# Sixteen accumulating weight transfers moved from the attention part into the recurrence of a hybrid residual block

## The chip, the cores and the metric

The kernel runs on one core of a Trainium2 chip. The metric is the device time of one execution in microseconds (us), lower is better. Five engines work in parallel, each with an instruction stream of its own: TensorE (PE in the profile, PEld for its weight loads), VectorE (DVE), ScalarE (ACT), GpSimd (POOL) and SyncE (SP). SP, ACT and POOL also issue DMA transfers. An instruction that has to wait for a semaphore holds up everything behind it on its engine.

## The reference, cut to what matters

One residual block over 1024 tokens of width 1024, in float32:

```python
xn = rmsnorm(x, norm1_g[layer])
u = xn @ w_in[layer]          # q,k,v (3x512), f,i,q,g of HGRN2 (4x512), two gates (2x1024)
...
o_sb = stick_breaking_attention(q_sb, k_sb, v_sb)                    # 8 heads of 64
o_hg = rmsnorm(hgrn2(silu(q_hg), k_hg, i_hg, log_f), hg_norm_g) * silu(g_hg)   # 4 heads of 128
g_a = sigmoid(gate_sb + bg[:D_MODEL])
g_b = sigmoid(gate_hg + bg[D_MODEL:])
merged = g_a * (o_sb @ w_o_sb) + g_b * (o_hg @ w_o_hg)
h = x + merged @ w_out
h = h + square(relu(rmsnorm(h, norm2_g) @ w_ff1)) @ w_ff2
return rmsnorm(h, final_g)
```

## The kernel before, in words

Everything is one long program on one core. Float32 products are made of three matmuls on a high and a low part, so most operands are split first: ACT copies the high part (`hi_copy`, line 157), DVE subtracts it from the original (`lo_sub`, line 162). All matmuls go through one helper (line 129), transposes through another (132).

Several large products (gates, output projections, MLP) are computed by Strassen-like schemes with fewer block products, which need sums of weight blocks. Some of these sums are made ahead by DMA alone, in HBM: a transfer on POOL's queue copies one block to a scratch tensor, and a later one adds a second block to it (`accum_op`). There are three such sets, each a Python generator that issues one transfer per step:

- `out_weight_sums`: four sums of W_OUT in `tw`, 16 copies and then 16 adds of 256 KB (line 1365);
- `sb_weight_sums`: four sums of W_OSB in `tv`, 8 transfers of 512 KB (line 1629), where the third and the fourth sum are built on `tv[1]` and the one made from it;
- `gate_weight_sums`: the gates' fourth sum in `tg4` (called `tg` in the profile), the sum of four blocks of W_IN: 4 copies and 12 adds of 512 KB (line 1377). It is read by SP's loads of the units `wga0` to `wga7`, much later.

The stages in order: norm and transposes of x (0 to 80 us), attention (about 80 to 326 us), the HGRN2 recurrence (about 323 to 550 us), gates, output projection, MLP.

**Attention** is a loop over 64 items (8 heads, 8 query blocks each). In each item ACT computes `rm`, the sigmoid of the scores (line 840), two items ahead; DVE scans it (859); PE transposes it to `pw`; ACT and DVE split that to `wTh` and `wTl`; PE multiplies with the values (`po`), and ACT evacuates to `osb` (934). Matmuls of the projections fill PE in between (`st.advance`). Beside that, `input_sums` lets DVE build sums of the input in `xs`, which POOL's queue stores to `sx` (1538); tiles of 128x1024 (`rm` of the larger blocks, `xs`, weights and others) share one pool of 40 slots, so a new `rm` can wait until the store of an old `xs` has landed. POOL also issues the transfers that copy QH and QL to the other partitions (730) and, once per head, an add of the two halves of `osb` (941); it also clears parts of `wTh` and `wTl` (892). SP stores `osb` of the last head to `od` (952).

At each item the chain of the three sets takes one step, `if i % 16 != 0: next(wsums, None)`; each transfer is placed behind `scored[0]`, the latest sigmoid of the scores, by an ordering that asks for no semaphore (`NOSYNC`): it only says where the instruction stands.

**The recurrence** goes over four heads. `hg_levels(h)` does seven levels of halves; each level ends with the product of the decays, `hg_level[0] = mul(right, right, left)` (DVE, line 170, `pp<-pp` in the profile), and PE computes the level's scores `sl` from keys `ksl` and `q`. `hg_tail(h)` computes the outputs; POOL makes the inverse roots from `hss` there (266, 270), and DVE multiplies by them (`hon`). PE is filled with projections again: first `pji` from W_IN's columns of `i`, whose weight comes in four quarters `wir`, loaded by SP and split to `wih` and `wil`.

Of the kernel before, what the change touches and what calls it, by code (L numbers as in the profile page):

```python
# [16 lines left out]
AX = mybir.AxisListType  # L17
PSUM = bass.MemoryType.PSUM
NOSYNC = mybir.DependencyInfo(mybir.DependencyClass.NoSync, mybir.DependencyReason.DATA)

P = 128
T = 1024
# [18 lines left out]
def kernel(  # L41
# [19 lines left out]
    nc = tc.nc  # L61
# [32 lines left out]
    def dram(name, shape):  # L94
        return scratch.tile(shape, F32, tag=name, name=name)
# [10 lines left out]
    def after(ins, earlier):  # L106
        if earlier is not None and earlier.ins is not ins.ins:
            tc.add_manual_dep(ins.ins, earlier.ins.name, NOSYNC, reason="issue order")
        return ins
# [710 lines left out]
    turn_lo, scored = [None], [None]  # L820

    def scores(h, qb):
        open_block("main")
        nk = (qb + 1) * P
        QH, QL, KS = qk[h]
        rm = zs[h, qb] = slot_n(f"rm{h}_{qb}", nk)
        step = 320 if nk == 640 else 512
        for s0 in range(0, nk, step):
            m = min(nk - s0, step)
            n = max(m, 256)  # L830
            z = bank(f"z{h}_{qb}_{s0}")
            for i, Q in enumerate((QH, QL)):
                matmul(
                    z[:, :n],
                    Q[:, qb * P : (qb + 1) * P],
                    KS[:, s0 : s0 + n],
                    start=i == 0,
                    stop=i == 1,
                )
            scored[0] = nc.scalar.activation(  # L840
                rm[:, s0 : s0 + m], z[:, :m], AF.Sigmoid, scale=-0.125
            )
# [7 lines left out]
    def weights(h, qb):  # L850

        nk = (qb + 1) * P
        rm = zs[h, qb]
        parts = ((512, nk), (0, 512)) if qb == NT - 1 else ((0, nk),)
        for i, (a, b) in enumerate(parts):
            rr = rm[:, a:b][:, ::-1]
            sc = nc.vector.tensor_tensor_scan(  # L859
                out=rr,  # L860
                data0=rr,
                data1=bits[:, 1024 - nk + a : 1024 - nk + b][:, ::-1],
                initial=rm[:, b : b + 1] if i else 0.0,
                op0=ALU.mult,
                op1=ALU.max,
            )
            if (h, qb) == items[0]:
                after(sc, masked[0])
            if i == 1 or (qb == 5 and h in (2,)):
                after(sc, turn_lo[0])  # L870
# [85 lines left out]
    hg_sum, hg_level = [None], [None]  # L956
# [397 lines left out]
    def out_block(i, j):  # L1354
        return W_OUT[i * 512 : (i + 1) * 512, j * 512 : (j + 1) * 512]

    def out_weight_sums():
        b11, b12, b21, b22 = (out_block(i, j) for i in range(2) for j in range(2))
        plain = ((1, b11), (3, b12), (2, b22), (4, b21))
        summed = ((1, b12), (3, b22), (2, tw[1]), (4, tw[2]))  # L1360
        for op, ways in ((ALU.bypass, plain), (ALU.add, summed)):
            for i, src in ways:
                for r in range(4):
                    rs = slice(r * P, (r + 1) * P)
                    after(nc.gpsimd.dma_start(tw[i][rs], src[rs], accum_op=op), scored[0])
                    yield

    tg4 = dram("tg4", [512, D])

    def gate_weight_sums():  # L1370
        for op, i, c0 in (
            (ALU.bypass, 0, C_GA), (ALU.add, 0, C_GB), (ALU.add, 1, C_GA), (ALU.add, 1, C_GB),
        ):
            for r in range(4):
                rs = slice(r * P, (r + 1) * P)
                src = W_IN[i * 512 + r * P : i * 512 + (r + 1) * P, c0 : c0 + D]
                after(nc.gpsimd.dma_start(tg4[rs], src, accum_op=op), scored[0])
                yield

    def gate_bias(which, cb):  # L1380
# [150 lines left out]
    def input_sums():  # L1531


        def step(out, a, b, op):
            after(nc.vector.tensor_tensor(out=out, in0=a, in1=b, op=op), turn_lo[0])

        def stored(m, kp, t):
            nc.gpsimd.dma_start(sx[m][kp], t)

        for kp in range(2):  # L1540
            (h00, l00), (h01, l01), (h10, l10), (h11, l11) = (
                [t.bitcast(F32) for t in xn.t[i, 2 * j + kp]] for i in range(2) for j in range(2)
            )
            s = slot(f"xs{kp}")
            step(s, h00, h10, ALU.subtract)
            yield
            step(s, s, l00, ALU.add)
            yield
            step(s, s, l10, ALU.subtract)
            stored(7, kp, s)  # L1550
            yield
            yield
            step(s, s, h11, ALU.add)
            yield
            after(
                nc.vector.scalar_tensor_tensor(
                    out=s, in0=s, scalar=-1.0, in1=l11, op0=ALU.mult, op1=ALU.subtract
                ),
                turn_lo[0],
            )  # L1560
            stored(6, kp, s)
            s4 = slot(f"xs4{kp}")
            yield
            step(s4, s, h01, ALU.add)
            yield
            step(s4, s4, l01, ALU.add)
            stored(3, kp, s4)
            yield
            step(s, s, h00, ALU.add)
            yield  # L1570
            step(s, s, l00, ALU.add)
            stored(5, kp, s)
            yield
# [41 lines left out]
    def sb_block(i, j):  # L1615
        return W_OSB[i * 256 : (i + 1) * 256, j * 512 : (j + 1) * 512]

    def sb_weight_sums():
        for t, op, src in (
            (1, ALU.bypass, sb_block(0, 0)),  # L1620
            (3, ALU.bypass, sb_block(0, 1)),
            (1, ALU.add, sb_block(0, 1)),
            (3, ALU.add, sb_block(1, 1)),
            (2, ALU.bypass, tv[1]),
            (2, ALU.add, sb_block(1, 1)),
            (4, ALU.bypass, tv[2]),
            (4, ALU.add, sb_block(1, 0)),
        ):
            after(nc.gpsimd.dma_start(tv[t], src, accum_op=op), scored[0])
            yield  # L1630
# [1005 lines left out]
    n_first = 4  # L2636
    n_fill = n_first + 14 * NHS
    ready = deque()
    wsums = chain(out_weight_sums(), sb_weight_sums(), gate_weight_sums())
    insums = input_sums()  # L2640
    done = 0
    for i, it in enumerate(items):
        if i + 1 < len(items):
            weights(*items[i + 1])
        if i + 2 < len(items):
            st.finish(j_qk[items[min(i + 4, len(items) - 1)][0]])
            scores(*items[i + 2])
        if i < 2:
            v_moves()
        if i % 16 != 0:  # L2650
            next(wsums, None)
        if i > 2 and i % 5 > 1:
            next(insums, None)
        want = n_first + (i + 1) * (n_fill - n_first) // len(items)
        st.advance(want - done, j_q[2])
        done = want
        before = ready.popleft() if ready else None

        def between():
            if before:  # L2660
                values(*before)

        r = turn(*it, between)
        if i == len(items) - 2:
            attended[0] = turn_lo[0]
        if it[1] != NT - 1:
            between()
        if r:
            ready.append(r)
# [9 lines left out]
    for h in range(NHG + 1):  # L2679
        lev = hg_levels(h) if h < NHG else iter(())  # L2680
        tail = hg_tail(h - 1) if h > 0 else iter(())
        upto = (j_i, j_sb[0], j_raw[1], j_raw[6], j_held)[h]
        going, turned = True, False
        while going:
            going = False
            for g in (lev, tail):
                if g is tail and h == 1 and turned and going and st.pos < j_i:
                    continue
                turned = turned or g is tail
                if next(g, StopIteration) is not StopIteration:  # L2690
                    going = True
                    owed += FILL[h]
                    for step in range(int(owed)):
                        st.advance(1, upto)
                        while soon:
                            soon.pop(0)()
                    owed -= int(owed)
        if h + 1 < NHG:
            st.finish(max(j_f[h + 1], j_q[h + 1]))
# [102 lines left out]
```

## Time and profile before

| | us |
|---|---|
| median of 3 runs | 1419.32 (1418.46 to 1420.83) |
| the profiled execution, its own time | 1421.75 |
| its span, first to last instruction | 1420.0 |
| PE busy | 1406.0 (99%) |
| DVE busy | 1066.9 (75%) |
| ACT busy | 667.8 (47%) |
| POOL busy | 164.4 (12%) |
| mean granted clock of PE | 0.997 |

Times in the views are counted from the span's start. A timeline row reads: start, busy time, engine, line, operation, output<-inputs, shape, count, and in square brackets how long the engine had stood idle before it and what ended that. In a view of one tile, a transfer's row gives its issue (duration, first and last start), and the line on landing the time from issue to landing. PEclk is the clock that the throttle granted, 1.00 being full speed.

### The profile page before, as it was taken

The page shows a single profiled execution, that of the slowest core. Times are in us where ns is not written, and L with a number is a line of the kernel's source. Part 1 is how long each engine was busy: PE and PEld are TensorE (multiplying, and loading weights), DVE is VectorE, ACT ScalarE, POOL GpSimd, SP SyncE. Part 2 cuts the span into 40 slices and gives each one's busy share as a digit, 9 for nine tenths or more (in the row PEclk, how much of TensorE's full clock was granted, in tenths as well). Part 3 has the DMA queues.
Part 4 walks back from the last instruction along what each step waited for, and adds up shares of the span by engine and source line. Part 5 has one row for each costly group of instructions (what it writes and reads, how often), then busy time and mean ns, then how long its engine had stood idle before and what let it go on. Part 6 is the DMA issues. An engine that isn't in the chain of part 4 may idle for free.

```text
span 1420.0 us, 18679 instructions
## 1 busy us (share of the span) xinstructions
PE 1406.0 (99%) x6824; PEld 1181.1 (83%) x6824; DVE 1066.9 (75%) x1463; ACT 667.8 (47%) x1147; POOL 164.4 (12%) x318
## 2 busy tenths in 40 slices
PE   9999999999999999999999999999999999999997
PEld 8888788888888888888888888888888888888886
DVE  6678887668578968987788897676666657768765
ACT  6455455554244555433334754445444443433343
POOL 3023343310001111000000300000000000000041
PEclk9999999999999999999999999999999999999999
DMA  7357778864213668364585514444346964776824
GB/s 252 83 141 201 150 142 195 211 149 134 86 56 105 215 222 264 129 215 156 165 294 194 185 59 164 163 163 149 137 143 244 355 255 160 270 278 241 282 91 176
DMA packets 169556, 258.18 MB, mean 182 GB/s; under 512 B 31404, under 2 KB 92376, under 8 KB 169432
## 3 DMA queue, kind: packets, MB, share of 16 engines
q1 hardware_dynamic: 148280, 196.15, 40.9%
q0 software_dynamic: 16320, 50.34, 13.8%
q10 hardware_dynamic: 4864, 10.49, 2.1%
q8 instruction: 54, 0.88, 0.3%
q14 instruction: 38, 0.31, 0.1%
HBM read 186.69 MB, written 84.94 MB: 191 GB/s over the span
## 4 chain that ended last, share of the span: by engine, by line
PE 95%; DVE 1%; ACT 1%; DMA 1%; issue 1%; SPq 0%; POOL 0%; POOLq 0%; DVEq 0%
PE pm L129 21%; PE pX L129 9%; PE pW L129 6%; PE pY L129 6%; PE pjqk L129 5%; PE gY L129 4%; PE gX L129 4%; PE pga L129 4%; PE pjf L129 3%; PE pji L129 3%; PE pyh L129 3%; PE pjq L129 3%; PE pys L129 3%; PE po L129 3%; PE pwX L129 2%; PE z L129 2%
## 5 line engine op out<-in xcount | busy, mean ns | idle before, releaser
L859 DVE TENSOR_TENSOR_SCAN rm<-rm,bits 128x512 f32<-128x512 f32 (+6 forms) x72 | 87.4, 1221 | 29.7 <-ACT rm L840 28.8
L157 ACT CAST whid<-w 128x1024 fp32r<-128x1024 f32 x30 | 31.6, 1054 | 154.1 <-PE pm L129 83.2
L129 PE MATMUL pm<-whid,sh 128*128 128x512 f32 x240 | 93.4, 389 | 0.0
L129 PE MATMUL pm<-wlod,sh 128*128 128x512 f32 x240 | 93.4, 389 | 0.0
L129 PE MATMUL pm<-whid,sl 128*128 128x512 f32 x240 | 93.4, 389 | 0.0
L129 PE MATMUL pm<-tl,sh 128*128 128x512 f32 (+1 forms) x210 | 81.3, 387 | 0.0
L129 PE MATMUL pm<-th,sl 128*128 128x512 f32 (+1 forms) x210 | 81.3, 387 | 0.0
L129 PE MATMUL pm<-th,sh 128*128 128x512 f32 (+1 forms) x210 | 81.3, 387 | 0.0
L162 DVE TENSOR_TENSOR wlod<-w,whid 128x1024 fp32r<-128x1024 f32 x30 | 36.7, 1223 | 53.6 <-ACT whid L157 53.6
L157 ACT CAST wTh<-pw 128x512 fp32r<-128x512 f32 (+2 forms) x96 | 43.8, 483 | 57.9 <-PE pw L132 54.2
L2413 POOL TENSOR_SCALAR fss<-fss 128x1 f32<-128x1 f32 x8 | 4.4, 552 | 562.0 <-ACT fsc L2408 561.5
L162 DVE TENSOR_TENSOR sl<-sa,sh 128x1024 fp32r<-128x1024 f32 x56 | 68.3, 1219 | 0.4 <-ACT sh L157 0.3
L162 DVE TENSOR_TENSOR wTl<-pw,wTh 128x512 fp32r<-128x512 f32 (+2 forms) x96 | 50.4, 546 | 21.8 <-ACT wTh L157 20.7
L157 ACT CAST sh<-sa 128x1024 fp32r<-128x1024 f32 x56 | 57.2, 1046 | 9.0 <-DMA sa<-ad 9.0
L129 PEld LDWEIGHTS pm<-wlod,sh 128*128 128x128 f32 x240 | 45.1, 188 | 9.5
L129 PEld LDWEIGHTS pm<-whid,sl 128*128 128x128 f32 x240 | 45.1, 188 | 9.3
L129 PEld LDWEIGHTS pm<-whid,sh 128*128 128x128 f32 x240 | 45.0, 187 | 9.4
L129 PE MATMUL pX<-sqh,t1l 128*128 128x512 f32 x128 | 49.9, 390 | 0.0
L129 PE MATMUL pX<-sql,t1h 128*128 128x512 f32 x128 | 49.9, 390 | 0.0
L129 PE MATMUL pX<-sqh,t1h 128*128 128x512 f32 x128 | 49.8, 389 | 0.0
L840 ACT ACTIVATE rm<-z 128x512 f32<-128x512 f32 (+3 forms) x96 | 44.5, 501 | 8.4 <-DMA sx<-xs 5.7
L129 PEld LDWEIGHTS pm<-th,sh 128*128 128x128 f32 x210 | 39.5, 188 | 8.1
(985 smaller groups left out, 4415.2 us busy)
## 6 DMA issues: line engine op xcount, KB each, us to landing
w<-in_w_ff_dram SPq DMA_DIRECT2D x72, 512.0 KB, 5.1
sa<-ad SPq DMA_DIRECT2D x52, 512.0 KB, 6.7
tg<-in_w_in_dram POOLq DMA_DIRECT2D x16, 512.0 KB, 9.1
ad<-a SPq DMA_DIRECT2D x32, 256.0 KB, 4.3
ad<-s SPq DMA_DIRECT2D x16, 512.0 KB, 2.8
tw<-in_w_out_dram POOLq DMA_DIRECT2D x24, 256.0 KB, 5.6
pr<-pd SPq DMA_DIRECT2D x10, 512.0 KB
x<-in_x_dram SPq DMA_DIRECT2D x8, 512.0 KB, 11.3
```

What stands on the lines that cost most here:

```text
L129: return pe(nc.tensor.matmul(*a, **k))
L157: hi_last[0] = after(in_turn("act", nc.scalar.copy(dst, src)), hi_behind[0])
L162: nc.vector.tensor_tensor(out=dst, in0=src, in1=hi.bitcast(F32), op=ALU.subtract),
L840: scored[0] = nc.scalar.activation(rm[:, s0 : s0 + m], z[:, :m], AF.Sigmoid, scale=-0.125)
L859: sc = nc.vector.tensor_tensor_scan(out=rr, data0=rr, data1=bits[:, 1024 - nk + a : 1024 - nk + b][:, ::-1], initial=rm[:, b : b + 1] if i ...
L2413: nc.gpsimd.tensor_scalar(out=ssq, in0=ssq, scalar1=1.0 / D, scalar2=EPS, op0=ALU.mult, op1=ALU.add)
```

## The change

The chain in the attention loop now holds only the first two sets, and takes a step at five items of eight, instead of fifteen of sixteen: 40 transfers over 64 items. The third set, the sixteen transfers of `tg4`, is stepped in the recurrence, once after each step of `hg_levels` (in the second head also of `hg_tail`) as soon as there is a level's product. Each now waits for the latest product by a semaphore (`SYNC`), where it only stood behind a sigmoid before.

```diff
+SYNC = mybir.DependencyInfo(mybir.DependencyClass.Sync, mybir.DependencyReason.DATA)
...
                 src = W_IN[i * 512 + r * P : i * 512 + (r + 1) * P, c0 : c0 + D]
-                after(nc.gpsimd.dma_start(tg4[rs], src, accum_op=op), scored[0])
+                tc.add_manual_dep(
+                    nc.gpsimd.dma_start(tg4[rs], src, accum_op=op).ins,
+                    hg_level[0].ins.name, SYNC, reason="pace",
+                )
                 yield
...
-    wsums = chain(out_weight_sums(), sb_weight_sums(), gate_weight_sums())
+    wsums = chain(out_weight_sums(), sb_weight_sums())
+    gsums = gate_weight_sums()
...
-        if i % 16 != 0:
+        if i % 8 not in (0, 3, 6):
             next(wsums, None)
...
                 if next(g, StopIteration) is not StopIteration:
                     going = True
+                    if hg_level[0] and (g is lev or h == 1):
+                        next(gsums, None)
                     owed += FILL[h]
```

On PE, DVE, ACT and SP the instructions and their order are the same as before. Only POOL's stream differs. First, POOL in the middle of attention, from the add of the second head's `osb` (issued at 144.5 us before) to the store `sx` (151.3 us) and the QL copy behind it. Before:

```order
L941 DMA osb_1424<-osb_1424 64x1024
L1365 DMA tw<-in_w_out_dram 128x512
L730 DMA QH_1528<-QH_1528 64x512
L892 MEMSET wTh_0_0_1673 128x128
L892 MEMSET wTl_0_0_1674 128x128
L1365 DMA tw<-in_w_out_dram 128x512
L730 DMA QL_1529<-QL_1529 64x512
L892 MEMSET wTh_3_4_1617 128x128
L892 MEMSET wTl_3_4_1618 128x128
L1365 DMA tw<-in_w_out_dram 128x512
L1538 DMA sx_153<-xs_1045 128x1024
```

The same place now:

```order
L942 DMA osb_1420<-osb_1420 64x1024
L1366 DMA tw<-in_w_out_dram 128x512
L731 DMA QH_1523<-QH_1523 64x512
L893 MEMSET wTh_0_0_1668 128x128
L893 MEMSET wTl_0_0_1669 128x128
L1366 DMA tw<-in_w_out_dram 128x512
L731 DMA QL_1524<-QL_1524 64x512
L893 MEMSET wTh_3_4_1612 128x128
L893 MEMSET wTl_3_4_1613 128x128
L1542 DMA sx_153<-xs_1044 128x1024
```

One transfer of `tw` ahead of the store has gone. Fifteen of them stood ahead of this piece before, so its three were the 16th to the 18th, a copy and two adds; now ten stand ahead, and its two are the 11th and the 12th, both copies.

Second, POOL at the end of attention, from the add of the seventh head's `osb` to the first roots of the recurrence. Before:

```order
L941 DMA osb_3093<-osb_3093 64x1024
L1377 DMA tg_150<-in_w_in_dram 128x1024
L892 MEMSET wTh_0_0_3321 128x128
...
L1377 DMA tg_150<-in_w_in_dram 128x1024
L892 MEMSET wTh_3_4_3274 128x128
...
L1377 DMA tg_150<-in_w_in_dram 128x1024
L892 MEMSET wTh_2_4_3442 128x128
...
L941 DMA osb_3419<-osb_3419 64x1024
L266 TENSOR_SCALAR hss_0_4157<-hss_0_4157 128x4
```

And now:

```order
L942 DMA osb_3077<-osb_3077 64x1024
L1633 DMA tv_159<-in_w_o_sb_dram 256x512
...
L1633 DMA tv_160<-tv_159 16x8192
...
L1633 DMA tv_160<-in_w_o_sb_dram 256x512
...
L1633 DMA tv_161<-tv_160 16x8192
L1633 DMA tv_161<-in_w_o_sb_dram 256x512
L942 DMA osb_3400<-osb_3400 64x1024
L1379 DMA tg_150<-in_w_in_dram 128x1024 x16
L267 TENSOR_SCALAR hss_0_4157<-hss_0_4157 128x4
```

The last transfers of `tv`, each of which builds on the one before, now stand ahead of the last head's `osb`, and all sixteen of `tg` between it and the roots. The sixteen were issued between 252.1 and 302.0 us before.

## The prediction

> **What bounds the kernel now.** I read the page first: busy times, then the chain that ended last, then the table of transfers.
>
> ```profile
> PE 1406.0 (99%) x6824; PEld 1181.1 (83%) x6824; DVE 1066.9 (75%) x1463; ACT 667.8 (47%) x1147; POOL 164.4 (12%) x318
> ...
> PE 95%; DVE 1%; ACT 1%; DMA 1%; issue 1%; SPq 0%; POOL 0%; POOLq 0%; DVEq 0%
> ...
> sx<-xs POOLq DMA_DIRECT2D x8, 512.0 KB, 4.1
> ```
>
> TensorE (PE) carries 95% of the chain. Its order is the same after the change, so the change can give only the time in which PE stands still or runs on a low clock: 1420.0 - 1406.0 = 14 us, much of it at the two ends. I therefore cut the attention part into pieces of 5 us and looked for the ones where PE is not busy throughout (columns: stretch, length, busy time, granted clock, DMA share, GB/s).
>
> ```profile
> 160.00:165.00 5.00, 4.41 (x23) 1.00 0.97 152
> 165.00:170.00 5.00, 4.02 (x23) 1.00 0.27 45
> 170.00:175.00 5.00, 3.82 (x16) 0.69 0.86 170
> 175.00:180.00 5.00, 5.00 (x31) 0.97 0.73 157
> ```
>
> One place stands out. PE idles 0.59 + 0.98 + 1.18 = **2.75 us** between 160 and 175, and then the clock is reduced: (1 - 0.69) x 5 + (1 - 0.97) x 5 = **1.70 us** of lost work. The last line of the same view for 80 to 340, which follows, shows that PE lost 260.00 - 257.01 = 2.99 us there in all, so all but 0.24 us in this place. The timeline names the waits, first on PE, then on ScalarE (ACT) and VectorE (DVE).
>
> ```profile
> sum 260.00, PE 257.01; mean PE 4.94
> ```
>
> ```profile
> 161.41 0.50 PE L129 MATMUL z<-KS,QH 128*128 128x512 f32 x1 [0.18 <-ACT rm L840]
> 163.02 0.50 PE L129 MATMUL pjq<-xnh,wq0h 128*128 128x512 f32 x1 [0.41 <-ACT osb L934]
> 171.18 0.39 PE L129 MATMUL po<-wTl,V 128*128 128x256 f32 x1 [2.17 <-DVE wTl L162]
> ```
> ```profile
> 154.89 0.36 ACT L934 ACTIVATE osb<-po,v_end 128x128 f32<-128x128 f32 x1
> 160.92 0.77 ACT L840 ACTIVATE rm<-z 128x320 f32<-128x320 f32 x2 [5.67 <-DMA sx<-xs]
> ...
> 161.72 1.49 DVE L859 TENSOR_TENSOR_SCAN rm<-rm,bits 128x640 f32<-128x640 f32 x1 [4.27 <-ACT rm L840]
> ```
>
> ACT, which was free at 155.25, stood 5.67 us until the store `sx<-xs` had landed, because the new `rm` takes the slot of `xs`. DVE then stood 4.27 us for ACT, worked from 161.72 on what had piled up, and PE waited for both. The three waits of PE, 0.18 + 0.41 + 2.17 = 2.76 us, are all of its idle time here. So the question is why this store was late.
>
> **Part 1: thinner queue in attention.** The store stands on the queue of GpSimd (POOL) behind transfers of the weight sums. Their landings, and those of quieter places:
>
> ```profile
> L1365 POOL DMA_DIRECT2D tw<-in_w_out_dram x1: 1163/1163/1163, 146.5 to 146.5; - x1
> DMA to landing us min/median/max: 9.6/9.6/9.6
> L1365 POOL DMA_DIRECT2D tw<-in_w_out_dram x1: 897/897/897, 149.0 to 149.0; - x1
> DMA to landing us min/median/max: 9.6/9.6/9.6
> L1538 POOL DMA_DIRECT2D sx<-xs x1: 591/591/591, 151.3 to 151.3; - x1
> DMA to landing us min/median/max: 9.6/9.6/9.6
> ```
> ```profile
> L1365 POOL DMA_DIRECT2D tw<-in_w_out_dram x2: 526/528/531, 127.0 to 127.9; - x2
> DMA to landing us min/median/max: 5.6/5.7/5.8
> L1538 POOL DMA_DIRECT2D sx<-xs x1: 560/560/560, 133.0 to 133.0; - x1
> DMA to landing us min/median/max: 3.0/3.0/3.0
> ```
>
> The landings are 146.5 + 9.6 = 156.1, 149.0 + 9.6 = 158.6 and 151.3 + 9.6 = 160.9: in the order of issue, 2.3 to 2.5 us apart, as of one queue that is worked off in turn. The issue at 149.0 is gone from this place after the change. The one at 146.5 is the 17th of its kind before, an adding one (the first 16 copy), and the 12th after, a copying one; two copies in a row, at 127.0 and 127.9, landed only about 0.9 us apart. Bounds for the landing of the store: at the latest 160.9 - 2.5 = 158.4 (only the missing transfer counts), at the earliest 151.3 + 3.0 = 154.3 (the fastest of its kind). I take 158.4 - 2 = about 156.5, since an adding transfer becomes a copy as well. ACT then starts 2.5 (late end), 4.4 (mine) or 5.67 us (early end) sooner. PE idled 2.76 us, so the late end leaves 0.26 us of idle and the other two none. Saved: **2.76 us** (2.5 to 2.76).
>
> The low clock follows that idle time, in the very next piece. I price it as gone with it: **1.70 us** (0 to 1.70). Here a rule of the Trainium skill differs: TensorE: Matmul & The Clock Gate, Part 1, says that the clock falls to half after at least one idle window of about 3.4 us. The trace shows 0.69 after a longest wait of 2.17 us, so the measurement decides. By that rule the dip would not be the wait's doing, and the sum would lack this term; that is a rival below.
>
> The rest of attention carries fewer transfers per unit of time than before: 40 over 64 items instead of 56 over the first 60. I price it at zero, since PE lost only the 0.24 us there. If a lump forms elsewhere, the price is that of the lump at 160: 4.46 us.
>
> **Part 2: the chain at the end of attention.** The eight sums of W_OSB move to the last two heads; some wait for the one before, and `osb` of the last head stands behind them on POOL.
>
> ```profile
> 231.36 0.52 POOL L1629 DMA_DIRECT2D tv<-tv  x1 [1.03 <-DMA tv<-in_w_o_sb_dram]
> ...
> 251.02 0.90 POOL L1629 DMA_DIRECT2D tv<-in_w_o_sb_dram  x1 [3.04 <-DMA tv<-tv]
> ...
> 326.97 0.82 POOL L941 DMA_DIRECT2D osb<-osb  x1 [16.38 <-ACT osb L934]
> ```
>
> From the first copy of a sum to the last add took 19.7 us before. After, that chain starts behind the previous head's `osb`, issued at 299.8, so at about 301.4, and ends at 321. `osb` waits for ACT until 326.97 anyway: 6 us of cover, cost zero. If the chain took over 26 us, each further us would hold `osb`, then SP's store of it, then the loads behind that.
>
> **Part 3: sixteen transfers in the recurrence.** They touch HBM alone, and POOL had nothing to do there for 74.86 us:
>
> ```profile
> 394.21 0.17 DVE L170 TENSOR_TENSOR pp<-pp 128x8 f32<-128x8 f32 x1
> ...
> 402.66 0.19 POOL L266 TENSOR_SCALAR hss<-hss 128x4 f32<-128x4 f32 x1 [74.86 <-ACT hon L1288]
> ...
> 465.38 0.45 SPq L137 DMA_DIRECT2D wga0r<-tg  x1
> ```
>
> The last product that any of them can wait for ends at 394.4, and with an issue of 0.9 us POOL is free at 395.3, 7.4 us ahead of `hss`, the first that is queued behind; were it late, DVE's `hon` would be. The slowest of these transfers took 12.8 us to land (last row below), so the sum is whole by about 408, 57 us ahead of the load that reads it. No PE, ACT, DVE or SP instruction is added. Cost zero each.
>
> What is not covered is a collision. The first product ends when SP issues the last quarter of `wi`, which ACT and DVE split on a nearly full DVE:
>
> ```profile
> 332.67 0.69 DVE L170 TENSOR_TENSOR pp<-pp 128x512 f32<-128x512 f32 x1
> 332.78 0.37 SPq L137 DMA_DIRECT2D wir<-in_w_in_dram  x1
> 336.26 1.06 ACT L157 CAST wih<-wir 128x1024 fp32r<-128x1024 f32 x1
> 337.54 1.22 DVE L162 TENSOR_TENSOR wil<-wir,wih 128x1024 fp32r<-128x1024 f32 x1
> 344.37 0.72 DVE L170 TENSOR_TENSOR q<-q,pp 128x512 f32<-128x512 f32 x1
> ...
> 345.42 0.38 PE L129 MATMUL sl<-q,ksl 128*128 128x128 f32 x2
> ```
> ```profile
> 255.00:260.00 5.00, 5.00 (x25) 1.00 1.06 303
> ...
> DMA to landing us min/median/max: 6.9/9.1/12.8
> ```
>
> DVE works without a gap from 337.54 to 345.09, and PE takes that `q` at 345.42: 0.33 us of slack, and 0.22 between ACT's cast (ending at 337.32) and DVE. The first `tg` moves 524 KB; at the 303 GB/s seen when such copies ran before, that is 1.7 us of all engines. If all of it goes ahead of the rest of `wi`, the cast is up to 1.7 us late, and PE waits 1.7 - 0.55 = 1.15 us; if the load was well landed, 0. I take **+0.6 us**, the middle, since the trace doesn't show how long before 336.26 that quarter had landed. A wait of this size cost no clock at 163 (0.41 us).
>
> **Sum**, against the profiled execution's 1421.75 us: -2.76 - 1.70 + 0.6 = -3.86, so 1417.9. The median of the runs, 1419.32, lies 2.43 below that execution; I apply the same difference, 1419.32 - 3.86 = **1415.5**. The ends: -2.76 - 1.70 + 0 = 1414.9, and -2.5 - 1.70 + 1.15 = 1416.3.
>
> **Rivals.**
> *The clock dips anyway.* The low clock starts at about 172, not in the idle time but behind it; if something else sets it, the gain is 2.76 - 0.6 = 2.16, time 1417.2. Against it: in 260 us of attention it fell only here. The clock rule above speaks for it. 10%.
>
> *The lump moves.* The store is freed and another transfer is late in its place (the adding ones now stand from 180 on), or unprofiled runs, which are 2.4 us shorter, don't have the wait. Then nothing is gained: 1419.32 + 0.6 = 1419.9. For it: the margin, ACT's 5.67 us for PE's 2.76, shows how thinly covered these waits are; against it, the four transfers of these sums issued between 179 and 182 held up nothing before. 22%.
>
> *The recurrence waits (slower).* The `wi` load is served after the whole first `tg`, whose landing takes 9.1 us at the median: 333.4 + 9.1 = 342.5 instead of 336.26, 6.2 us late, less 0.55 of slack is 5.7 of PE idle, with the clock 7.4, against 4.46 gained: 1419.32 + 2.9 = 1422.3. It eats the gain from 3.3 us of lateness on. For it: at 151 a store behind such transfers landed 5.5 us later than its median. Against: `wi` comes on SP's queue, not on POOL's. The Trainium skill, DMA: Bandwidth & Descriptors, Queues, rings and completion order, says that a DMA engine takes turns between queues by packets; by that rule the lateness stays near the 1.7 us above. 13%.
>
> **How the numbers follow.** My forecast has 55%, its own range being 1414.0 to 1417.0 (the ends above, widened by 0.8 us, about half the spread of the runs shown). About 0.2%, 2.8 us, can be told from no change here, so faster means below 1416.5: most of my forecast, 50%. The same: its upper end, the dipping clock and the moved lump, 37%. Slower: 13%. The range must take in the moved lump and leaves out the slow rival: 1413.8 to 1420.4.
>
> **What the profile after would show.** Right: ACT's wait for `sx` near 155 under 2 us, PE busy 5.00 of 5.00 from 160 to 175, clock 1.00 there, the store landing in about 5 us; sixteen issues of `tg` between 328 and 392 (all is 4 us earlier), each behind a product; `hss` still waiting for ACT. Part 3's price would stand as a PE wait for DVE's `q` near 341. It is wrong if PE waits elsewhere in attention for ACT or DVE behind a transfer, if the clock falls again, or if `wih` or `wil` is over 3 us later in its place.

## The result and the profile after

The changed kernel's median is **1417.43 us** (1416.70 to 1418.68, 22 runs) and the kernel before ran at 1420.49 us beside it (1418.46 to 1421.29, 22 runs). The ratio is 0.9981, 95% interval [0.9974, 0.9987]: about 3 us faster. The three runs known before the change, with 1419.32 us, were on the low side: the same kernel, run in four more batches beside the experiments below, gave 1420.65, 1420.87, 1420.77 and 1421.07 us. The profiled execution took 1418.08 us (1421.75 before), its span is 1416.2 us and the mean clock 0.998.

First the page, then the pieces of 5 us around the place in question (stretch, length, PE busy, clock, DMA share, GB/s), and the last line of the same view over 80 to 340 us.

```profile
PE 1404.1 (99%) x6824; PEld 1179.5 (83%) x6824; DVE 1066.8 (75%) x1463; ACT 667.2 (47%) x1147; POOL 166.3 (12%) x318
```
```profile
160.00:165.00 5.00, 5.00 (x28) 1.00 0.10 35
165.00:170.00 5.00, 4.69 (x28) 1.00 0.64 159
170.00:175.00 5.00, 5.00 (x33) 1.00 0.48 156
```
```profile
sum 260.00, PE 259.46; mean PE 4.99
```

The idle time of this place went from 2.75 to 0.31 us, the low clock from 1.70 to nothing, and PE lost 0.54 us in all between 80 and 340 where it had lost 2.99. The next two views show why: the landing of the store `sx`, by its tile, and ACT's timeline.

```profile
L1542 POOL DMA_DIRECT2D sx<-xs x1: 572/572/572, 151.2 to 151.2; - x1
...
DMA to landing us min/median/max: 3.9/3.9/3.9
```
```profile
154.84 0.36 ACT L935 ACTIVATE osb<-po,v_end 128x128 f32<-128x128 f32 x1
155.23 0.77 ACT L841 ACTIVATE rm<-z 128x320 f32<-128x320 f32 x2
```

The store landed 3.9 us after its issue, at 155.1, instead of 9.6. ACT's `rm` has no bracket any more: it starts behind `osb` without a wait (5.67 us before). PE's two longest waits that are left in these parts of the kernel are one in attention and one in the recurrence:

```profile
168.15 0.39 PE L130 MATMUL po<-wTl,V 128*128 128x256 f32 x1 [0.31 <-DVE wTl L163]
```
```profile
341.27 1.13 PE L130 MATMUL sl<-q,ksl 128*128 128x128 f32 x8 [0.29 <-DVE q L171]
```

On POOL the sixteen transfers stand where the order put them, and both instructions that could have been held, `osb` ahead of them and `hss` behind, still wait for ACT and not for the queue:

```profile
322.37 0.82 POOL L942 DMA_DIRECT2D osb<-osb  x1 [3.93 <-ACT osb L935]
329.07 0.56 POOL L1379 DMA_DIRECT2D tg<-in_w_in_dram  x1 [5.88 <-DVE pp L171]
...
391.18 0.81 POOL L1379 DMA_DIRECT2D tg<-in_w_in_dram  x1 [1.65 <-DMA tg<-in_w_in_dram]
398.60 0.19 POOL L267 TENSOR_SCALAR hss<-hss 128x4 f32<-128x4 f32 x1 [6.61 <-ACT hon L1289]
```

### The profile page after: what moved, and what is told of

The parts are those of the page before. It is cut to its first block, busy times and chain, and to the rows that moved or that the text cites. A ratio compares the mean times of both kernels' runs of the same rounds, so it can differ in the third digit from the quotient of the medians.

```text
span 1416.2 us, 18690 instructions
## 1 busy us (share of the span) xinstructions
PE 1404.1 (99%) x6824; PEld 1179.5 (83%) x6824; DVE 1066.8 (75%) x1463; ACT 667.2 (47%) x1147; POOL 166.3 (12%) x318
## 4 chain that ended last, share of the span: by engine, by line
PE 93%; DMA 2%; DVE 2%; ACT 1%; issue 1%; SPq 0%; POOL 0%; POOLq 0%; DVEq 0%
PE pm L130 21%; PE pX L130 9%; PE pW L130 6%; PE pY L130 6%; PE pjqk L130 5%; PE gY L130 4%; PE gX L130 4%; PE pga L130 4%; PE pjf L130 3%; PE pyh L130 3%; PE pys L130 3%; PE pji L130 3%; PE po L130 2%; PE pwX L130 2%; PE z L130 2%; PE pjq L130 2%
## 5 line engine op out<-in xcount | busy, mean ns | idle before, releaser
L130 PEld LDWEIGHTS pm<-tl,sh 128*128 128x128 f32 x210 | 39.5, 188 | 8.2
```

The source lines that it names most:

```text
L130: return pe(nc.tensor.matmul(*a, **k))
```

## The experiments

Two questions: is the whole gain the one late store, and what do the transfers cost in the recurrence? Times are medians; a ratio is to the kernel before, run on the same chip.

### Attention: the store and what stands ahead of it

**Two transfers fewer ahead of the store.** The kernel before, with the chain's step left out at two items; nothing goes to the recurrence.

```diff
-        if i % 16 != 0:
+        if i % 16 != 0 and i not in (18, 19):
             next(wsums, None)
```

> The kernel before, with the chain of all three sets left out at items 18 and 19 only: the two adding transfers ahead of the store sx near 151 us come two items later, all else stays in attention. Theory 1 (the whole gain comes from this one place): the store lands in about 4 us, ACT's wait near 155 is under 1 us, PE busy at least 4.6 of each 5 us from 160 to 175, clock 1.00 there, time 3 to 4 us under the kernel before, so as fast as the changed kernel or 0.3 us faster, since the recurrence pays nothing. Theory 2 (the gain comes from less traffic in the whole of attention, without the gates' sixteen): less than 1 us under the kernel before.

1417.45 us, ratio 0.9981 [0.9972, 0.9990]. ACT, and the one piece of 5 us between 160 and 180 in which PE had idle time:

```profile
154.99 0.77 ACT L840 ACTIVATE rm<-z 128x320 f32<-128x320 f32 x2
```
```profile
165.00:170.00 5.00, 4.69 (x29) 1.00 0.72 93
```

The store landed in 3.6 us. Two steps less in this place bring all that the change brings, and leave the same 0.31 us. ACT no longer waits for the store here, so that wait for `wTl` belongs to neither the store nor the change.

**One transfer fewer.** As above, with only `i != 19` left out.

> The kernel before, with the chain left out at item 19 only: one adding transfer less ahead of the store, the other one stays. Theory 1 with the late end of my bounds: the store lands about 2.3 us earlier than before (7.3 us after its issue instead of 9.6), ACT waits about 3.3 us, PE idles 0.2 to 0.5 us between 160 and 175, no low clock there; 2.3 us less idle and 1.7 us of clock, so 3.5 to 4 us under the kernel before. Theory 3 (the clock dips by itself): the low clock near 172 stays although PE idles under 0.5 us, and the time is only 2 to 2.5 us under the kernel before.

1418.32 us, ratio 0.9985 [0.9976, 0.9993].

```profile
158.37 0.77 ACT L840 ACTIVATE rm<-z 128x320 f32<-128x320 f32 x2 [3.40 <-DMA sx<-xs]
```
```profile
165.00:170.00 5.00, 3.98 (x25) 1.00 0.67 89
170.00:175.00 5.00, 5.00 (x33) 1.00 0.94 238
```

The store landed 7.3 us after its issue, 2.3 sooner. PE still idled 1.02 us, more than expected (the late end in the prediction had left 0.26), yet the clock stayed at 1.00. By its time alone, 2.3 us under the kernel before, the run would fit theory 3; the clock in the trace decides for theory 1. Here idle time and low clock come apart: 1.02 us of waiting costs no clock, and the 2.17 us before cost 1.70 us of it.

**The same transfers, two as copies.** `out_weight_sums` with the first two adds of its second part as plain copies; order and bytes as before.

```diff
-                    after(nc.gpsimd.dma_start(tw[i][rs], src[rs], accum_op=op), scored[0])
+                    if op is ALU.add and i == 1 and r < 2:
+                        after(nc.gpsimd.dma_start(tw[i][rs], src[rs], accum_op=ALU.bypass), scored[0])
+                    else:
+                        after(nc.gpsimd.dma_start(tw[i][rs], src[rs], accum_op=op), scored[0])
```

> The kernel before, with the first two adding transfers of the first W_OUT sum turned into copies at the same places (so these rows of that sum lack one block). It tells number from kind. If adding is what is slow: the store lands in 5 to 6 us, ACT waits about 1 us, time 3 to 4 us under the kernel before. If the number of transfers ahead of it counts: landing 8 to 9.6 us, ACT's wait 4 to 5.7 us, time within 1 us of the kernel before.

1417.52 us, ratio 0.9981 [0.9972, 0.9990]. The store's tile, and ACT:

```profile
L1541 POOL DMA_DIRECT2D sx<-xs x1: 575/575/575, 151.3 to 151.3; - x1
...
DMA to landing us min/median/max: 5.4/5.4/5.4
```
```profile
156.78 0.77 ACT L840 ACTIVATE rm<-z 128x320 f32<-128x320 f32 x2 [1.48 <-DMA sx<-xs]
```

With the number of transfers unchanged the landing falls from 9.6 to 5.4 us; with both of them away it was 3.6. So of the 6.0 us that the two cost the store, the adding is 4.2. ACT's remaining 1.48 us are covered.

**The move alone.** The changed kernel with the old pace in attention: the sixteen go to the recurrence, but the chain steps at fifteen items of sixteen.

```diff
-        if i % 8 not in (0, 3, 6):
+        if i % 16 != 0:
             next(wsums, None)
```

> The changed kernel with the old pace in attention (fifteen items of sixteen), so that the gates' sixteen transfers alone are moved. Theory 1: the lump ahead of the store is back as it was, ACT waits 5 to 6 us near 155, PE idles 2.5 to 3 us between 160 and 175, the clock falls to half for 3.4 us, and the recurrence costs 0.3 us: 0 to 0.5 us slower than the kernel before. Theory 2: 2 to 3 us faster than the kernel before.

1420.80 us, ratio 1.0002 [0.9993, 1.0011].

```profile
160.55 0.77 ACT L841 ACTIVATE rm<-z 128x320 f32<-128x320 f32 x2 [5.27 <-DMA sx<-xs]
```
```profile
165.00:170.00 5.00, 3.65 (x19) 1.00 0.41 55
170.00:175.00 5.00, 4.18 (x18) 0.68 0.84 193
```

The wait and the low clock are back. So taking sixteen transfers out of attention and putting them into the recurrence, both together, doesn't move the time; the slower pace, which thins the queue ahead of one store, does.

### The recurrence: what the pace is worth

**No waits for the products.** The changed kernel, the sixteen ordered as before but without a semaphore.

```diff
-                tc.add_manual_dep(
-                    nc.gpsimd.dma_start(tg4[rs], src, accum_op=op).ins,
-                    hg_level[0].ins.name, SYNC, reason="pace",
-                )
+                after(nc.gpsimd.dma_start(tg4[rs], src, accum_op=op), hg_level[0])
```

> The changed kernel with the sixteen gate transfers in the same places on POOL's queue, but ordered only, without the wait for a level's product; they are issued as fast as the queue and the adds' own order let them, from about 323 us on. Theory 1 (pacing spares the loads of the recurrence): eight or so transfers are in flight when the last quarter of wi is loaded at about 328 us, it lands 2 to 5 us later, and PE waits 2 to 5 us near 336 to 342, perhaps with a low clock: 2 to 6 us slower than the changed kernel. Rival (the loads get their share whatever stands on POOL's queue): PE waits under 1 us in the recurrence, within 1 us of the changed kernel.

1445.28 us, ratio 1.0172 [1.0158, 1.0186]: 27.9 us behind the changed kernel, far beyond what I expected. POOL now issues all sixteen between 323.1 and 358.2. ACT's splits of two weights that SP loads (`wi`, `wf3`), PE in one piece of 10 us, and the packets of the two queues from 324 to 350 us (q0 is POOL's, q1 is SP's):

```profile
340.84 1.04 ACT L158 CAST wih<-wir 128x1024 fp32r<-128x1024 f32 x1 [9.00 <-DMA wir<-in_w_in_dram]
360.86 1.04 ACT L158 CAST wf3h<-wf3r 128x1024 fp32r<-128x1024 f32 x1 [18.97 <-DMA wf3r<-in_w_in_dram]
```
```profile
350.00:360.00 10.00, 0.00 (x0) 0.65 1.07 214
```
```profile
q0 software_dynamic: 1454, 5.30, 89.0%
q1 hardware_dynamic: 950, 1.09, 14.0%
```

PE stands still from 350 to 360: it waits for DVE's `q`, which stands behind DVE's split of `wf3`, and these weights don't arrive. POOL's packets carry 5.30 MB / 1454 = 3.6 KB and take 0.890 x 26 x 16 / 1454 = 0.25 us of a DMA engine each; SP's carry 1.1 KB and take 0.06 us. That fits SP's packets waiting behind long ones, though no view shows the order of single packets.

**The same without the adding.** The sixteen unpaced, all as plain copies (`ALU.bypass` for `ALU.add` in `gate_weight_sums`).

> The changed kernel without the waits for the levels' products, as in the run that took 1445.3 us, but with all sixteen transfers as plain copies; three of the four blocks are left out of the gates' sum by this. Theory A: the adding holds the queues; copies of the same bytes at the 303 GB/s seen for them in attention are through in 8.4 MB / 303 GB/s = 28 us instead of some 45, ScalarE waits for the load of wf3 5 to 10 us instead of 19, and the time is 1420 to 1432 us. Theory B: any transfers issued without a pace take the turns of SP's loads, adding or not: ScalarE still waits 15 us or more for wf3 and the time is 1438 us or more.

1431.77 us, ratio 1.0077 [1.0060, 1.0094], within theory A's range. ACT's wait for `wf3`, and the queues in the same stretch:

```profile
349.82 1.04 ACT L158 CAST wf3h<-wf3r 128x1024 fp32r<-128x1024 f32 x1 [10.28 <-DMA wf3r<-in_w_in_dram]
```
```profile
q0 software_dynamic: 1889, 6.87, 77.3%
q1 hardware_dynamic: 2370, 1.81, 21.7%
```

Half of the 27.9 us is left (14.3). A copy's packet takes 0.773 x 26 x 16 / 1889 = 0.17 us, a third less, and SP's queue gets 1.81 MB through instead of 1.09. Adding doubles the harm; plain copies without a pace do the other half.

**The adding under the pace.** The changed kernel, all sixteen as plain copies, with their waits.

> The changed kernel with its sixteen transfers all as plain copies, the same bytes read and written at the same places; three of the four blocks are left out of the gates' sum by this. Theory A: an adding transfer holds the queues longer than a copy, so the load of wf3 comes sooner (ScalarE waited 3.9 us for it), the second store of v is read again sooner than 14.1 us after its issue, PE's 0.3 us wait for q goes, and the time is 0 to 0.6 us below the changed kernel, 1416.8 to 1417.6 us. Rival: the number of bytes is what delays them, waits and time stay as they are, 1417.4 us within 0.4.

1417.37 us, ratio 0.9977 [0.9967, 0.9987]. The landing of the sixteen as copies:

```profile
DMA to landing us min/median/max: 3.6/5.9/8.5
```

The median falls from 9.6 to 5.9 us, the second store of the values (next section) is read again after 8.8 us instead of 14.2, and PE has no wait for `q`; but the time, which fits theory and rival alike, is that of the changed kernel within 0.1 us. At this pace the adding is covered.

### The recurrence: where the transfers stand

**Start two products later, with two doubled.** The first two products pass without a transfer; at the 8th and 9th, two are issued each.

```diff
-                        next(gsums, None)
+                        paced += 1
+                        for _ in range(0 if paced < 3 else 2 if paced in (8, 9) else 1):
+                            next(gsums, None)
```

> The changed kernel with the first two products skipped, so that the first gate transfer waits for the third product (near 341 us) and two are issued at each of two later products. Theory 1: ACT's cast of the last wi quarter no longer waits for its load (0.40 us before), PE's wait of 0.29 us for q at 341 us is gone, time 0.2 to 0.4 us under the changed kernel, which is hardly to be told from it. Rival (that wait has another cause, say DVE's own order): the 0.29 us stays.

1422.03 us, ratio 1.0009 [1.0000, 1.0018]: 4.6 us slower than the changed kernel, and my expectation failed. PE's waits, then ACT: it stores the second half of the values (`vd<-v`) and reads it back in another order (`v<-vd`), with `pp<-pk` queued behind.

```profile
342.44 1.13 PE L130 MATMUL sl<-q,ksl 128*128 128x128 f32 x8 [1.52 <-DVE q L171]
382.61 2.07 PE L130 MATMUL sl<-q,ksl 128*128 128x128 f32 x8 [3.20 <-ACT pp L1247]
```
```profile
361.81 0.32 ACTq L1014 DMA_DIRECT2D vd<-v  x1
...
380.57 1.07 ACTq L1001 DMA_DIRECT2D v<-vd  x2
381.97 0.97 ACT L1247 COPY pp<-pk 128x512 f32<-128x512 f32 x2 [15.89 <-issue]
```
```profile
381.00:383.00 2.00, 0.39 (x2) 0.78 0.96 170
383.00:385.00 2.00, 2.00 (x10) 0.50 0.50 125
385.00:387.00 2.00, 2.00 (x9) 0.86 0.26 84
```

The store was read back only 18.8 us after its issue, and ACT stood in order behind that load ("issue" in the bracket: the profile shows nothing that it waited for). The same rows of the changed kernel, with the transposes that `pp` is made of:

```profile
L133 PE MATMUL pk<-ident,k x7: 270/273/273, 366.8 to 367.5; 128*128 128x128 f32 x7
```
```profile
360.22 0.32 ACTq L1014 DMA_DIRECT2D vd<-v  x1
...
374.37 1.08 ACTq L1001 DMA_DIRECT2D v<-vd  x2
375.77 0.97 ACT L1247 COPY pp<-pk 128x512 f32<-128x512 f32 x2 [10.84 <-PE sl L130]
```

There too ACT waited 10.84 us; the bracket names PE, but PE's transposes were done at 367.8, and ACT moves when the load goes out at 374.37, 14.2 us after the store's issue. In the changed kernel this wait just fits. In the kernel before, with no transfers here, store to load took 5.5 us:

```profile
362.89 0.32 ACTq L1013 DMA_DIRECT2D vd<-v  x1
...
368.42 1.08 ACTq L1000 DMA_DIRECT2D v<-vd  x2
```

In sum, PE's extra idle time (1.52 + 3.20 - 0.29 = 4.43) and half of its 2.9 busy us on the low clock (1.46) make 5.9 us; the spans differ by 6.0. (The medians differ by 4.6 us; the profiled execution, with 1423.96 us, was one of the slower of its eleven.) The 1.52 us are not the doing of these transfers, since the first of them was issued only at 343.2, when the wait had ended. They seem to come from the chain at the end of attention, Part 2 of the prediction:

```profile
328.30 0.50 SPq L953 DMA_DIRECT2D od<-osb  x1
```

The last `tv` was issued at 318.88 here, 317.56 in the changed kernel; `osb` behind it landed in 5.9 us instead of 4.5; SP's store of `osb` went out at 328.30 instead of 326.89 and the last `wi` load behind that store 0.7 us later; ACT waited 1.99 us for it instead of 0.40, and `q` and PE stand behind. In the trace of the doubled run below and in that of the copies above the last `tv` went out at 315.1 and 315.4, and `osb` landed in 4.0 us. That the late `tv` slows `osb` is read from these traces, not tested by a run.

Two runs take the edit apart.

**Later, not doubled.** The first two products skipped, one transfer at each product from then on.

> The changed kernel with the first two of its products skipped and one transfer with each product from the third on, none doubled (the run before this one doubled two, at the 8th and 9th products). Theory A: what cost 4.6 us there was the doubling, which put adding transfers ahead of the second store of v; ScalarE stood in order behind the load that waits for this store, 15.9 us, and TensorE waited 3.2 us for ScalarE's pp and then lost 1.7 us to a low clock. By A the store is read again within 14.1 us of its issue, as in the changed kernel (360.2 to 374.4), PE waits for no pp, and the time is within 1417.0 to 1419.0 us. Theory B: the later start itself is what costs (the transfers of the second head crowd each other later on): the wait for pp stays and the time is 1420.5 to 1422.5 us.

1417.32 us, ratio 0.9978 [0.9970, 0.9987].

```profile
359.86 0.32 ACTq L1014 DMA_DIRECT2D vd<-v  x1
...
373.72 1.08 ACTq L1001 DMA_DIRECT2D v<-vd  x2
```

13.9 us from store to load, no wait of PE between 320 and 410, and the time of the changed kernel.

**Doubled, not later.** None skipped, two transfers at the 8th and 9th products.

> The changed kernel with two transfers instead of one at the 8th and 9th products, and none skipped, so that the last two come two products sooner. Theory A: the doubling delays the second store of v as it did with the later start: ScalarE waits more than 14.5 us in front of pp, PE waits 2 to 4 us for pp, and the time is 1419.5 to 1422.5 us. Theory B: the doubling is harmless when nothing starts later; PE waits for no pp, 1416.8 to 1418.2 us.

1425.62 us, ratio 1.0040 [1.0026, 1.0054]: 8.2 us slower than the changed kernel, more than theory A had said.

```profile
359.69 0.32 ACTq L1014 DMA_DIRECT2D vd<-v  x1
...
376.64 1.08 ACTq L1001 DMA_DIRECT2D v<-vd  x2
```
```profile
378.69 1.16 PE L130 MATMUL sl<-q,ksl 128*128 128x128 f32 x8 [1.31 <-ACT pp L1247]
...
394.38 0.77 PE L130 MATMUL pkv<-v,pp 128*128 128x128 f32 x2 [4.55 <-DMA v<-vd]
```

From the ninth on, each transfer now comes one or two products sooner, and that is enough. Store to load takes 17.0 us, so PE waits 1.31 us for `pp`, less than theory A had said. Then PE waits 4.55 us more for the values themselves. The load, issued late, has the next transfers beside it (issued at 377.0, 381.6, 385.0 and 388.6) and three loads of `osr` on SP's queue; which of these delays it is not shown.

The delayed read-back of theory A is there in both doubled runs, and the later start alone costs nothing. What differs is how many transfers POOL issues between 355 and 367 us, around the store of `vd`: two in the changed kernel and in the run without doubling, five in the run with both changes and four in this one. Two copies in the same stretch let the store be read after 8.8 us, so kind counts as well as number. From store to load, less PE's wait for `pp`, the two doubled runs give 18.8 - 3.2 = 15.6 us and 17.0 - 1.3 = 15.7: by this estimate the changed kernel, with 14.2, is about 1.4 us away from paying.

## Why the prediction was right or wrong

**Part 1, the store.** The mechanism was right: ACT's wait for `sx` was the place, and one transfer fewer plus one copy in place of an add freed it. The landing came at 155.1 (said: about 156.5). The idle time saved is 2.44 us, not 2.76: the step that failed is "all of PE's idle time there is the store's". 0.31 us are DVE's own `wTl`, as the run with two transfers fewer shows. The price of the late end, 0.26 us of idle, was wrong as well: the run that sits nearest to it kept 1.02. Subtracting ACT's lateness from PE's idle time assumes that both shrink alike, and they don't. DVE's piled-up work, which lies between, is the likely reason.

**The low clock**, -1.70 us, was right and went with the wait. The rival that it dips anyway falls, although its 1417.2 us came nearer to the measured 1417.4 than the forecast's 1415.5; that is luck: no dip in the three attention runs that shorten PE's wait to 1.02 us or less, and a dip again in the move alone, with 2.17. The Trainium skill, TensorE: Matmul & The Clock Gate, Part 1, asks for an idle window of about 3.4 us; here 2.17 us of waiting was enough, so the measurement decides.

**The lump moves** (rival) didn't happen: 0.54 us of idle time in 260, and nothing new above 0.31.

**Part 2**, the end of attention, cost nothing in the changed kernel's profile, as said: the last `osb` waits for ACT. But the cover was thinner. From the first copy of a sum to the last add took 21.0 us instead of 19.7, which left 4.8 of the 6 us; and cover up to the issue of `osb` is not cover up to its landing. In the run with the later start the issue still waited 2.55 us for ACT, and yet the path that the prediction named, `osb`, SP's store, the loads behind, cost PE up to 1.52 us.

**Part 3, the recurrence.** `hss` was not held. The collision was priced at +0.6 us (0 to 1.15) and PE waited 0.29 us for `q`, in the place named. The load that came late was mostly that of `wf3`, which the prediction didn't count: ACT's split of it began 7.1 us after its issue, 4.7 before and 4.7 in the run with the first transfer only at 341.2, and DVE's split of it stands ahead of `q`. In the doubled run and in that of the copies, with the same first transfers, it was 6.2 and 6.3 us, and PE had no wait for `q`; so the 0.29 us is no fixed price.

What the prediction missed is the true danger. I looked for cover at `hss` and at the load of `wga0`, far away, and at the first `tg` against one load; the thin cover is ACT's, in `vd<-v` and `v<-vd`, of which I said nothing. It held with one transfer at a product and broke with two at two of them. (Without semaphores this place was spared: the last transfer went out at 358.2, `vd` was stored at 385.7 and read after 5.5 us.)

The slow rival was right in mechanism (SP's load starving), but at this pace it doesn't occur; without the pace it does, with 27.9 us. The bound of 1.7 us, all bytes of the first `tg` at 303 GB/s, held under the pace: ACT's split of the last `wi` quarter began 3.9 us after its load's issue, 3.5 before. With several transfers in flight it says nothing: ACT waited 9.0 us for the unpaced `wi`. The Trainium skill, DMA: Bandwidth & Descriptors, Queues, rings and completion order, says that a DMA engine takes turns between queues by packets. That is not against the run (950 packets of SP beside 1454 of POOL). But turns are not bytes: equal numbers of such packets, of 1.1 and 3.6 KB, would give SP a quarter of the bytes and a fifth of the time. Whether the profile's packets are those of the rule, no run shows.

**The sum.** Profile against profile it is -3.67 us (said: -3.86): 2.44 of idle time and 1.70 of clock are gained, 0.29 is lost in the recurrence, and PE idles 0.34 us more in the first 40 us, where both programs are the same. That makes 3.51; 0.16 stays unexplained. Two errors of size cancel, which is luck: 0.32 us less gained at the store and 0.31 us less paid in the recurrence. Against medians the term that was off is the base: 1419.32 was 1.17 us below the median of 22 runs, and subtracting from it gave 1415.5 where 1417.4 was measured. With 1420.49 the same sum gives 1416.6, within 0.8. The profiled execution before, 1421.75 us, lies above all 22 runs beside the change, so its waits may be larger than usual; that is not shown.

The forecast's own range, 1414.0 to 1417.0, misses 1417.4; the wide one, made to take in the moved lump, holds it. Half the spread of the runs shown, 1418.46 to 1420.83, is 1.2 us and not 0.8; widened by that, the range would have been 1413.7 to 1417.5.

## What to carry to other kernels

A background transfer is not free because its engine is idle; ask which store or load of the main work is in flight beside it, and who stands in order behind that one. An adding transfer cost 1.6 to 2 times a copy here (landing 9.6 against 5.9 us, time lost without a pace 27.9 against 14.3). Issuing two at a time at two places cost 8.2 us; one by one, the same sixteen cost 0.3 us at most. When a change moves many things, look for the single wait that ended last: leaving out two steps of a loop gave here the same 3 us as the whole change, while moving the sixteen gave none. And count the cover of a transfer up to its landing, not to its issue.

## What the runs showed of the hardware

**How long a wait lowers the clock.** PE's waits of 1.02, 1.31 and 1.52 us left the granted clock at 1.00. Waits of 2.17 (twice) and 3.20 us each brought about 3.4 us at half speed, and 4.55 us brought twice that, as the doubled run shows in pieces of 2 us: 0.64 + 2 + 2 + 2, and 0.16 in the next piece (clock 0.96), are 6.8 us at half speed.

```profile
391.00:393.00 2.00, 0.00 (x0) 0.84 1.08 266
393.00:395.00 2.00, 0.62 (x3) 0.50 1.02 217
395.00:397.00 2.00, 2.00 (x6) 0.50 0.47 111
397.00:399.00 2.00, 2.00 (x6) 0.50 0.24 57
```

The length of the wait alone doesn't settle it: in the unpaced copies 2.89 us, with 0.47 us more of waiting 0.8 us later, also brought 6.8 us (339.4 to 346.2).

The low clock does not start with the wait but later, even where PE works again by then, so it shows in the piece behind the one that caused it. In the eight places of these runs where it falls between 100 and 420 us it starts 2.1 to 4.3 us after the wait's beginning: 2.5 here (389.8 to 392.4), 2.7 in the run with the later start (379.4 to 382.1), 2.9 before (169.0 to 171.9), 3.2 in the move alone (168.6 to 171.8), 2.7 and 2.1 in the unpaced copies, 2.4 and 4.3 in the run without waits for the products.

**Adding transfers.** Under the pace the sixteen transfers of 512 KB, twelve of them adding, landed in 9.6 us at the median, with all as copies in 5.9; beside adding ones the 512 KB store of `v` was read back after 14.2 us, beside copies after 8.8 (359.92 to 368.69), beside none after 5.5.
